# Filter spectra spread over two projections, both forget gates projected before the values, three logarithms in a row, residual rows kept in PSUM behind the experts

## The chip, the cores and the metric

The kernel runs on one core of one Trainium2 chip, in one launch with float32 inputs and outputs. The metric is the device time of one execution in microseconds. Engines are named as the profile names them: PE is TensorE, DVE is VectorE, ACT is ScalarE, POOL is GpSimd and SP is the queue of SyncE that issues nearly all weight loads.

## The reference, cut to what matters

Two blocks follow one another on 256 tokens of width 1024. The change touches the first block only.

```python
h = concat([meta_tokens(16), x(256)])              # 272 rows
p = rms_norm(h) @ w_in                             # 8 column groups of 512
y_hy = hyena_mixer(p[:, :1536])                    # groups 0 to 2: short convolution, then two long ones
y_hg = hgrn2_mixer(p[:, 1536:])                    # q, f_fwd, f_bwd, values, g
h = h + concat([rms_norm(y_hy), y_hg]) @ w_out
h = h + hier_moe(rms_norm(h))                      # 64 experts, top 2, weights of 6 MB each
h = rms_norm(h)                                    # then the second block, two layers

# filter of one long convolution, as a spectrum
filt = (sin(...) @ w3) * window                    # 272 taps, forward and backward; the 0th taps are summed
spec = rfft(two_sided(filt))
# forget gate of one direction
f = lb + (1 - lb) * sigmoid(logit);  k = 1 - f;  lf = log(f)
```

## The kernel before, in words

**Projections.** The mixer (`_phase_a`) multiplies in float32 by splitting each operand into a high and a low part and adding three products. A weight tile of 128x8x512 (2 MB) is loaded by `_load_w` into a ring buffer, and `_split_w` makes the pair for one of its 8 chunks: ACT writes the high part (L183) and DVE the low part (L184). The pairs lie in four buffers named `wp`. `hyena_proj(i)` makes column group i turned, in four PSUM tiles `mh`, with 96 matmuls of 272 columns, and its convolution then takes one ACT and two DVE instructions for each of the four tiles (L352 to L354). `tok_proj` makes a group token by token (tiles `mm`), with 48 matmuls of 512 columns, and 16 more where the meta tokens are wanted.

**Filter spectra.** The loop at L397 runs for both convolutions. For each of three chunks of taps (the 16 odd taps first) and both halves there are two matmuls into a PSUM tile `fl`, one DVE multiplication with the window `wn` (L412), one ACT copy and one DVE subtraction (L414, L415; the odd taps go by L420 to L425). Five rows of the spectrum then take 7 matmuls each, the last one 14, and an ACT copy into `H`. One filter is 54 matmuls of 512 columns.

**Order.** The framework assigns instructions to each engine's queue from a priority by program order and a time plan made when the program is built. Each queue then runs strictly in the order written, and `_after` pins an instruction behind another one. In program order the steps are: group 0, both filters, group 1, `to_freq` and group 2, first inverse transform, `to_freq`, forward gate (`forget_proj(0)`), second inverse transform, q, `pss` (a sum of squares), values v, release of the left half of the SBUF (`left.close()`), backward gate (`forget_proj(1)`), four `core` calls of the recurrence, `g_proj`, `out_proj(0)`, `out_proj(1)`.

**Ring buffers.** Until `left.close()` all weight tiles share one ring of three buffers. `early()` then opens a second ring of two, `ring2`, and puts it in front, so that the next loads take ring2, ring2, ring, ring, ring. `_moe` sets its own order, [r, r2, r2, r3, r3, r, r], and loads 11 of the first expert group's 12 tiles (gate 0 to 3, up 0 to 3, down 0 to 3) in a chain in which each is pinned behind the one before it:

```python
first.append(load_g(x, 0, i, {3: spare[0], 4: spare[1], 9: spare[2], 10: spare[3]}.get(n)))
if n:
    _after(k, k.load, prev)
```

Gate 3, up 0, down 1 and down 2 have buffers of their own (`spare`). Gate 1 and gate 2 take ring2, up 3 and down 0 take the first ring.

**End of the experts.** In the last group of four experts the down projection runs in four parts with 14 warm-up matmuls on the identity behind each of the first three. `finish` then makes one product for each half row (tile `sc`), DVE adds it to the row `h` in SBUF (L1142), multiplies with the gain into `fan` (L1147, two of the four on POOL), ACT squares both (L1152), a few one-column instructions and a POOL power give the scale (L1155 to L1158), and DVE makes the normalised row `an` (L1169), which PE turns (`tp`, L1175) for the next projection `pt`.

Of the kernel before, what the change touches and what calls it, by code (L numbers as in the profile page):

```python
# [8 lines left out]
F32 = mybir.dt.float32  # L9
# [29 lines left out]
def _consts():  # L39
# [24 lines left out]
    z = np.concatenate([tt[:, None], np.cos(ang), -np.sin(ang)], 1).astype(f)  # L64
    zt = np.ascontiguousarray(z[perm].T)
    deltas = np.abs(np.linspace(math.log(1e-2) / 1.5, math.log(1e-2) / 0.3, W, dtype=f))
    win = np.exp((-tt[:, None] * deltas[None, :]).astype(np.float64)).astype(f)[perm]

    om = 2.0 * math.pi * (np.arange(L1) + 0.5) / NDFT
    px, pm = np.arange(NM, L1), np.arange(NM)  # L70
# [94 lines left out]
def _load_w(k, src, rows=8, t=None, parts=1, between=None):  # L165
    if t is None:
        p = k.rings.pop(0)
        k.rings.append(p)
        t = p.tile([128, 8, 512], F32, name="wring")
    dst = t if rows == 8 else t.rearrange("p (k m) n -> p k (m n)", k=rows)  # L170
    n = rows // parts
    for i in range(0, rows, n):
        k.load = k.nc.sync.dma_start(dst[:, i:i + n], src[:, i:i + n])
        if between and i in between:
            between[i]()
    return t
# [25 lines left out]
def _phase_a(k, A, early):  # L202
# [180 lines left out]
    first = norms[0]  # L383
    behind = filt[-1][1]

    nc.sync.dma_start(wn, A["c_win"])


    H = [pa.tile([128, 5, W], F32, name=f"H{o}") for o in range(2)]
    wz.append(_load_w(k, win_ap[:, :, W:2 * W]))  # L390
    load_w3(1)
    k.load_c1()
    sks = [sp.tile([80, W], F32R, name=f"sk{i}") for i in range(2)]
    for sk in sks:
        G.memset(sk.bitcast(F32), 0.0)
        _after(k, nc.scalar.copy(sk, sk.bitcast(F32)), ends[0])
    for o in range(2):  # L397
        if o:

            later = w3_sums(o)  # L400
            w3_pair()
        sd = [[sp.tile([128, 2, W], F32R, name=f"sd{n}{i}") for n in "hl"] + [sks[i]] for i in range(2)]
        tm = []
        for kt in (2, 0, 1):
            n = 128 if kt < 2 else NM
            for i, (sh, sl, sk) in enumerate(sd):
                ks = slice(kt * 128, kt * 128 + n)
                p = px([128, W], "fl")
                _mm(k, p[:n], hids[:, ks], wsh[:, i], True, False)
                _mm(k, p[:n], hids[:, ks], wsl[:, i], False, True)  # L410
                t = sp.tile([128, W], F32, name="sdt", bufs=2)
                V.tensor_tensor(t[:n], p[:n], wn[:n, kt], op=OP.mult)  # L412
                if kt < 2:
                    nc.scalar.copy(sh[:, kt], t)  # L414
                    V.tensor_tensor(sl[:, kt], t, sh[:, kt].bitcast(F32), op=OP.subtract)  # L415
                else:
                    tm.append(t)
            if kt == 2:

                V.tensor_tensor(tm[0][0:1], tm[0][0:1], tm[1][0:1], op=OP.add)  # L420
                V.tensor_scalar(tm[0][0:1], tm[0][0:1], 0.5, None, op0=OP.mult)
                for (sh, sl, sk), t in zip(sd, tm):
                    nc.scalar.copy(sk[0:16], t[:16])
                    nc.scalar.copy(sk[32:48], t[:16])
                    V.tensor_tensor(sk[64:80], t[:16], sk[0:16].bitcast(F32), op=OP.subtract)  # L425
        for r in range(5):
            m = 128 if r < 4 else 64
            p = px([128, W], "fl")
            parts = [(sd[r // 2], r * 128)] if r < 4 else [(sd[0], 512), (sd[1], 576)]
            for i, ((sh, sl, sk), c0) in enumerate(parts):  # L430
                c = slice(c0, c0 + m)
                for kt in range(2):
                    _mm3(k, p[:m], (Fs[:, 0, kt, c], Fs[:, 1, kt, c]), (sh[:, kt], sl[:, kt]), i + kt == 0, False)
                _mm(k, p[:m], Fss[:, c], sk, False, i == len(parts) - 1)
            nc.scalar.copy(H[o][:m, r], p[:m])

    Fm = const(pa, "fm", [128, 2, 640], later)
    Fms = const(pa, "fmst", [80, 576], later)
# [101 lines left out]
    zk = hc.tile([80, W], F32R, name="zk")  # L540
    G.memset(zk.bitcast(F32), 0.0)
    nc.scalar.copy(zk, zk.bitcast(F32))
    hyena_proj(1)

    nw = hp.tile([128, W], F32, name="nw")
    k.bcast(nw, A["hgrn_norm"])
# [10 lines left out]
    def bound(n):  # L557

        l = VC[n].rearrange("p (r c) -> p r c", r=2)
        e, m = hp.tile([128, 2, 4], F32, name="lbe"), hp.tile([128, 4], F32, name="lbm")  # L560
        V.tensor_tensor(m, l[:, 0], l[:, 1], op=OP.max)
        for r in range(2):
            V.tensor_tensor(e[:, r], l[:, r], m, op=OP.subtract)
        nc.scalar.activation(e, e, AF.Exp)
        V.tensor_tensor(m, e[:, 0], e[:, 1], op=OP.add)
        V.reciprocal(m, m)
        V.tensor_tensor(m, m, e[:, 0], op=OP.mult)
        dg = hp.tile([128, 4, 128], F32, name="dg", tag="fe")
        V.tensor_tensor(dg, k.ident[:, None, :].to_broadcast([128, 4, 128]), m[:, :, None].to_broadcast([128, 4, 128]), op=OP.mult)
        p = px([128, 4, 128], "lb")  # L570
        for c in range(4):
            _mm(k, p[:, c], k.one, dg[:, c], c == 0, c == 3)
        p = p.rearrange("p a b -> p (a b)")
        lb = hp.tile([128, 2, W], F32, name="lb")
        for r, sg in enumerate((0.5, -0.5)):
            nc.scalar.activation(lb[:, r], p, AF.Copy, scale=sg, bias=0.5)
        return lb

    def forget(p, n, lb, ko, fo):
        e = hp.tile([n, W], F32, name="fe")  # L580
        nc.scalar.activation(e, p, AF.Tanh, scale=0.5)
        V.tensor_tensor(e, e, lb[:n, 1], op=OP.mult)
        V.tensor_tensor(fo, lb[:n, 0], e, op=OP.add)
        V.tensor_tensor(ko, lb[:n, 1], e, op=OP.subtract)

    def forget_proj(d):
        lb = bound(("lb_fwd", "lb_bwd")[d])
        P = tok_proj(hcols(1 + d), d == 0)
        for t in range(2):
            forget(P[t], 128, lb, kk[d][:, t], lf[d][:, t])  # L590
        if d == 0:
            meta_sum(mk, P[2])
            forget(mk, NM, lb, mk, ml)
            x = nc.scalar.activation(ml, ml, AF.Ln)
        y = nc.scalar.activation(lf[d], lf[d], AF.Ln)
        if d == 0:
            _after(k, y, x)

    Y = to_freq(uT[0], H[0])
    hyena_proj(2)  # L600
    for m in range(4):
        p = from_freq(Y, m)
        u = uT[0][:, m]
# [10 lines left out]
    for m in range(4):  # L614
# [6 lines left out]
        gc = VC["hyena_norm"][:, m:m + 1]  # L621
        nc.scalar.activation(hyT[0][:, m], y, AF.Copy, scale=gc)
        V.scalar_tensor_tensor(hyT[1][:, m], y, gc, hyT[0][:, m].bitcast(F32), op0=OP.mult, op1=OP.subtract)
    P = tok_proj(hcols(0), False)
    for t in range(2):
        e = _sigmoid(k, hp, P[t], W, tag="fe")
        V.tensor_tensor(q[:, t], P[t], e, op=OP.mult)
    pss = ps.tile([128, 2], F32, name="pss", tag="mm")
    for m in range(4):
        for t in range(2):  # L630
# [3 lines left out]
    V.tensor_copy(sst, pss)  # L634
    _rsqrt_mean(k, rh, sst, W, po, tag="rsh")

    P = tok_proj(hcols(3), True)
    for t in range(2):
        nc.scalar.copy(v[:, t], P[t])
    meta_sum(mv, P[2])  # L640
    hy1.close()
    left.close()
    psA.close()
# [168 lines left out]
            logits(1, n, range(4))  # L812
            squares(1, n)

    forget_proj(1)

    p = px([128, W], "ep")
    _mm(k, p[:NM], B3[0][2][32:48, 32:48].bitcast(F32), ml, True, True)
# [59 lines left out]
def _moe(k, A, ctx, ps):  # L878
# [230 lines left out]

    def finish(gT, y):


        fan = k.mp.tile([128, 2, D], F32, name="fan", tag="hn")
# [20 lines left out]
        k.pre = P, pairs  # L1136

        def scatter(t, n):
            p = ps.tile([128, W], F32, name="sc", tag="px")
            m = q(_mm(k, p, gT[:, t], y[n], True, True))  # L1140
            hs = k.h[:, t, n * W:(n + 1) * W]
            q(V.tensor_tensor(hs, p, hs, op=OP.add))  # L1142
            return m

        def gained(eng, t, n):
            cs = slice(n * W, (n + 1) * W)
            q(eng.tensor_tensor(fan[:, t, cs], k.h[:, t, cs], k.gains[:, 1, cs], op=OP.mult))  # L1147

        def squares(t, n):
            for j, src in enumerate((k.h, fan)):  # L1150
                sq = mo.tile([128, W], F32, name="nsq")
                q(ACT.activation(sq, src[:, t, n * W:(n + 1) * W], AF.Square, scale=D ** -0.5, accum_out=f(t, 2 * j + n)))  # L1152

        def scale(t):
            q(V.tensor_scalar(f(t, 5), f(t, 0), f(t, 1), EPS, op0=OP.add, op1=OP.add))  # L1155
# [29 lines left out]
                q(_mm(k, P[t], k.ahl[0][:, 1, c, HS(t)], pairs[i][0][:, j], False, c == 7))  # L1185

        scatter(0, 0)
        gained(V, 0, 0)
        scatter(0, 1)
        gained(V, 0, 1)  # L1190
        scatter(1, 0)
        q(warm_up(WS, scatter(1, 1), "mm"))
        squares(0, 0)
        squares(0, 1)
        gained(G, 1, 0)
        scale(0)
        hi(0)
        squares(1, 0)
# [2 lines left out]
        hi(1)  # L1201
        turned(0)
        mm(0, 0)
        gained(G, 1, 1)
        lo(1)
        mm(0, 1)
        hi(2)
# [9 lines left out]
        for t in range(2):  # L1217
            q(G.tensor_tensor(f(t, 4), f(t, 5), k.mhalf, op=OP.pow))
            q(ACT.activation(k.h[:, t], fan[:, t], AF.Copy, scale=f(t, 4)))

    JS = [slice(j * SLOTS, (j + 1) * SLOTS) for j in range(EP)]
    extra = {4: (0, 0), 6: (0, 1), 8: (1, 0), 10: (1, 1)}
    for g in range(k.ngroups):
# [55 lines left out]
        hT = mb.tile([128, 4, 128], F32, name="hT")  # L1279
        nc.scalar.copy(hT, p)  # L1280
        P = [ps.tile([128, W], F32, name="dn", tag="mm") for _ in range(2)]
        wm = None
        for f in range(4):
            for n in range(2):
                for j in range(EP):
                    m = _mm(k, P[n][JS[j]], hT[:, f, JS[j]], w(2, f, j, n), f == 0, f == 3)
                    if wm:
                        _after(k, m, wm)
            if g == k.ngroups - 1 and f < 3:
                wm = warm_up(WD, m, "px")  # L1290
        y = [mb.tile([128, W], F32, name="ye") for _ in range(2)]
        for n in range(2):
            (V.tensor_copy if n else nc.scalar.copy)(y[n], P[n])  # L1293
        if g == k.ngroups - 1:
            finish(gT, y)
            return
        for t in range(2):
            for n in range(2):
# [862 lines left out]
```

## Time and profile before

| what | value |
|---|---|
| median of 3 runs | 2095.82 us (2094.42 to 2096.31) |
| profiled execution: time | 2094.49 us |
| profiled execution: span | 2092.7 us |
| instructions | 24267 |
| PE busy | 1847.5 us, 88% |
| DVE busy | 919.5 us, 44% |
| ACT busy | 652.1 us, 31% |
| DMA | 593.92 MB, mean 284 GB/s |
| mean granted TensorE clock | 0.945 of full speed |

The span runs from the first to the last instruction on the core. Times inside it are counted from its start. Busy shares are averages over three stages: the mixer up to about 260 us, the experts from there to about 1200 us, and the second block to the end.

### The profile page before, as it was taken

Reading aid. Unit: us, or ns where it says so; the run is one execution under the profiler, and the core shown is the slowest. Engines: PE = TensorE matmul, PEld = TensorE weight load, DVE = VectorE, ACT = ScalarE, POOL = GpSimd, SP = SyncE. Lnnn points to the kernel's source line nnn. Section 1 sums busy time; section 2 is a strip of 40 time slices with the busy share of each in tenths; the row PEclk is TensorE's granted clock in tenths of the full one; section 3 lists DMA queues with packets and bytes.
Section 4 is the critical chain, followed back from the end, with each engine's and each line's share of the span. In section 5 each row is a group of like instructions: output and inputs, shape, how many; then the busy total and the mean of one; then the engine's idle time right before and its main releaser. Section 6 shows DMA issues by size and latency. Waiting matters only on the chain.

```text
span 2092.7 us, 24267 instructions
## 1 busy us (share of the span) xinstructions
PE 1847.5 (88%) x10132; PEld 1212.4 (58%) x10132; DVE 919.5 (44%) x1521; ACT 652.1 (31%) x976; POOL 69.6 (3%) x89
## 2 busy tenths in 40 slices
PE   8999987678787787876777799999999999999998
PEld 7877832224232331322222379898788788888886
DVE  6886621021111100111111176756666957756756
ACT  5556400002000100000000154546544645446444
POOL 2000000000000000000000020000000100000000
PEclk9999998789899998988988899999999999999999
DMA  8244899999999999999999954455454355454541
GB/s 278 95 159 146 305 398 428 424 404 415 428 423 428 424 427 428 423 427 423 428 426 428 392 182 161 161 180 182 167 185 166 133 190 179 165 180 171 178 159 55
DMA packets 123265, 593.92 MB, mean 284 GB/s; under 512 B 5951, under 2 KB 7264, under 8 KB 101008
## 3 DMA queue, kind: packets, MB, share of 16 engines
q1 hardware_dynamic: 119008, 583.66, 70.3%
q10 hardware_dynamic: 3376, 5.45, 0.8%
q0 software_dynamic: 768, 3.21, 0.4%
q8 instruction: 82, 1.34, 0.3%
q14 instruction: 31, 0.25, 0.0%
HBM read 591.26 MB, written 1.05 MB: 283 GB/s over the span
## 4 chain that ended last, share of the span: by engine, by line
PE 55%; DMA 21%; DVE 3%; issue 1%; ACT 1%; POOL 0%; ACTq 0%; SPq 0%; DVEq 0%; POOLq 0%
PE pt L141 23%; PE gu L141 10%; DMA wring<-in_w_up 8%; DMA wring<-in_w_down 7%; DMA wring<-in_w_gate 6%; PE pT L141 5%; PE pu L141 5%; PE dn L141 5%; PE pw L141 1%; PE ca L141 1%; DVE wp L184 1%; PE ov L141 1%; PE mk L141 1%; PE xp L141 1%; PE warm L141 0%
## 5 line engine op out<-in xcount | busy, mean ns | idle before, releaser
L141 PE MATMUL pt<-wp,ahl 128*128 128x512 f32 x2160 | 516.8, 397 | 1.7 <-DVE wp L184 1.7
L184 DVE TENSOR_TENSOR wp<-wring,wp 128x1024 fp32r<-128x1024 f32 (+1 forms) x368 | 405.7, 1112 | 238.5 <-ACT wp L183 231.2
L183 ACT ACTIVATE wp<-wring 128x1024 fp32r<-128x1024 f32 (+1 forms) x368 | 353.1, 966 | 350.5 <-PE pt L141 176.5
L141 PEld LDWEIGHTS pt<-wp,ahl 128*128 128x128 f32 x2160 | 403.2, 188 | 93.6 <-DVE wp L184 2.5
L141 PE MATMUL gu<-wring,xg 128*32 128x512 f32 x2016 | 322.4, 680 | 122.9 <-DMA wring<-in_w_up 101.3
L141 PEld LDWEIGHTS gu<-wring,xg 128*32 128x32 f32 x2016 | 75.0, 122 | 341.9 <-issue 163.7
L141 PE MATMUL dn<-wring,hT 128*32 128x512 f32 x992 | 186.0, 686 | 65.7 <-DMA wring<-in_w_down 49.9
L141 PEld LDWEIGHTS dn<-wring,hT 128*32 128x32 f32 x992 | 44.2, 118 | 194.2 <-issue 98.3
L1275 DVE SCALAR_TENSOR_TENSOR hh<-th,gu 128x512 f32<-128x512 f32 x16 | 16.9, 1055 | 308.5 <-PE gu L141 308.5
L1293 DVE COPY ye<-dn 128x512 f32<-128x512 f32 x16 | 11.1, 692 | 276.8 <-PE dn L141 276.8
L141 PEld LDWEIGHTS pT<-ahl,wp 128*128 128x128 f32 x960 | 115.6, 189 | 0.5
L141 PE MATMUL pT<-ahl,wp 128*128 128x256 f32 x960 | 115.8, 283 | 0.0
L1280 ACT COPY hT<-hp 128x512 f32<-128x512 f32 x16 | 9.4, 586 | 295.0 <-PE hp L1278 295.0
L141 PE MATMUL pu<-wp,yTh 128*128 128x512 f32 x320 | 98.9, 397 | 0.8 <-ACT yTh L1459 0.6
L1271 ACT ACTIVATE th<-gu 128x512 f32<-128x512 f32 x16 | 9.5, 596 | 250.5 <-PE gu L141 250.5
L1293 ACT COPY ye<-dn 128x512 f32<-128x512 f32 x16 | 9.4, 586 | 242.0 <-PE dn L141 242.0
L141 PEld LDWEIGHTS xp<-oh,hn 128*128 128x128 f32 x512 | 64.0, 200 | 31.1 <-issue 25.7
L141 PE MATMUL xp<-oh,hn 128*128 128x128 f32 x512 | 68.3, 288 | 7.8 <-PEq L1064 4.6
L141 PEld LDWEIGHTS pu<-wp,yTh 128*128 128x128 f32 x320 | 58.7, 188 | 15.6 <-ACT yTh L1459 3.5
L1272 DVE SCALAR_TENSOR_TENSOR th<-th,gu 128x512 f32<-128x512 f32 x16 | 11.0, 687 | 126.1 <-ACT th L1271 126.1
L141 PE MATMUL pu<-wp,yTl 128*128 128x512 f32 x160 | 61.0, 395 | 0.2
L141 PE MATMUL sc<-ye,gT 128*128 128x512 f32 x128 | 59.3, 606 | 0.0
(539 smaller groups left out, 1995.8 us busy)
## 6 DMA issues: line engine op xcount, KB each, us to landing
wring<-in_w_up SPq DMA_DIRECT2D x73, 2048.0 KB, 18.5
wring<-in_w_in SPq DMA_DIRECT2D x63, 2048.0 KB, 7.8
wring<-in_w_gate SPq DMA_DIRECT2D x63, 2048.0 KB, 19.4
wring<-in_w_down SPq DMA_DIRECT2D x62, 2048.0 KB, 20.9
wring<-in_w_out SPq DMA_DIRECT2D x6, 2048.0 KB, 7.9
wring<-in_w_mem_kv SPq DMA_DIRECT2D x4, 2048.0 KB, 17.0
spare<-in_w_down SPq DMA_DIRECT2D x2, 2048.0 KB, 9.6
wring<-in_w_in SPq DMA_DIRECT2D x4, 512.0 KB, 6.2
```

The costliest lines, as they stand in the source:

```text
L141: return k.nc.tensor.matmul(out, a, b, start=start, stop=stop, skip_group_check=True, **kw)
L183: ih = k.nc.scalar.activation(hi, w[:, a:b], AF.Copy)
L184: il = (eng or k.nc.vector).tensor_tensor(lo, w[:, a:b], hi.bitcast(F32), op=OP.subtract)
L1271: nc.scalar.activation(th, P[0], AF.Tanh, scale=0.5)
L1272: V.scalar_tensor_tensor(th, th, 1.0, P[0], op0=OP.add, op1=OP.mult)
L1275: V.scalar_tensor_tensor(hh, by_f(th), 0.5, by_f(P[1]), op0=OP.mult, op1=OP.mult)
L1280: nc.scalar.copy(hT, p)
L1293: (V.tensor_copy if n else nc.scalar.copy)(y[n], P[n])
```

## The change

- The 0th window value is halved in the constant, and the instruction that halved the sum of the 0th taps goes. The window is loaded behind group 1's weights instead of ahead of them, in two parts, without the rows that are empty.
- The loop over the filters becomes `filter_steps(o)`, eight pieces (three chunks of taps, now with the odd ones last, and five rows). `hyena_proj(1)` runs one piece of filter 0 at each of its 8 chunks, `hyena_proj(2)` one of filter 1.
- q's projection moves ahead of the first inverse transform, and both `bound` calls ahead of it. `forget_proj(1)` moves ahead of v, and `pss` behind v.
- `forget` computes (tanh - 1) times half of 1 - lb, then f = 1 + e and k = -e. `bound` makes one tile instead of two.
- The three logarithms run in a row behind the last tanh.
- In the last expert group, four matmuls on the identity put the rows of `h` into PSUM (`waiting_rows`), in place of eight warm-up matmuls in each of two parts. `finish` adds its products to them there, and `fan` and the squares read PSUM. All four `fan` products run on DVE.

```diff
-    nc.sync.dma_start(wn, A["c_win"])
     wz.append(_load_w(k, win_ap[:, :, W:2 * W]))
+    nc.sync.dma_start(wn[:, :2], A["c_win"][:, :2])
+    nc.sync.dma_start(wn[:NM, 2], A["c_win"][:NM, 2])
...
-    for o in range(2):
-        if o:
-
-            later = w3_sums(o)
-            w3_pair()
+    def filter_steps(o):
...
-                V.tensor_scalar(tm[0][0:1], tm[0][0:1], 0.5, None, op0=OP.mult)
...
+        steps = [lambda kt=kt: taps(kt) for kt in (0, 1, 2)] + [lambda r=r: row(r) for r in range(5)]
+        return dict(enumerate(steps))
+
+    hyena_proj(1, filter_steps(0))
+
+    later = w3_sums(1)
+    w3_pair()
+    hyena_proj(2, filter_steps(1))
...
-        lb = hp.tile([128, 2, W], F32, name="lb")
-        for r, sg in enumerate((0.5, -0.5)):
-            nc.scalar.activation(lb[:, r], p, AF.Copy, scale=sg, bias=0.5)
+        lb = hp.tile([128, W], F32, name="lb", bufs=2)
+        nc.scalar.activation(lb, p, AF.Copy, scale=-0.5, bias=0.5)
...
-        V.tensor_tensor(e, e, lb[:n, 1], op=OP.mult)
-        V.tensor_tensor(fo, lb[:n, 0], e, op=OP.add)
-        V.tensor_tensor(ko, lb[:n, 1], e, op=OP.subtract)
+        V.scalar_tensor_tensor(e, e, 1.0, lb[:n], op0=OP.subtract, op1=OP.mult)
+        V.tensor_scalar(fo, e, 1.0, None, op0=OP.add)
+        V.tensor_scalar(ko, e, -1.0, None, op0=OP.mult)
...
     Y = to_freq(uT[0], H[0])
-    hyena_proj(2)
+    lbs = [bound(n) for n in ("lb_fwd", "lb_bwd")]
+    P = tok_proj(hcols(0), False)
+    for t in range(2):
+        e = _sigmoid(k, hp, P[t], W, tag="fe")
+        V.tensor_tensor(q[:, t], P[t], e, op=OP.mult)
...
+    x = forget_proj(1)
+    for a in (ml, lf[0], lf[1]):
+        x = _after(k, nc.scalar.activation(a, a, AF.Ln), x)
+
+    P = tok_proj(hcols(3), True)
     for t in range(2):
-        e = _sigmoid(k, hp, P[t], W, tag="fe")
-        V.tensor_tensor(q[:, t], P[t], e, op=OP.mult)
+        nc.scalar.copy(v[:, t], P[t])
+    meta_sum(mv, P[2])
     pss = ps.tile([128, 2], F32, name="pss", tag="mm")
...
-    forget_proj(1)
...
         def scatter(t, n):
-            p = ps.tile([128, W], F32, name="sc", tag="px")
-            m = q(_mm(k, p, gT[:, t], y[n], True, True))
-            hs = k.h[:, t, n * W:(n + 1) * W]
-            q(V.tensor_tensor(hs, p, hs, op=OP.add))
-            return m
+            return q(_mm(k, rows[t, n], gT[:, t], y[n], False, True))
...
+    def waiting_rows(rows, t, behind):
+
+        for n in range(2):
+            p = rows[t, n] = ps.tile([128, W], F32, name="sc", tag="px")
+            behind = _after(k, _mm(k, p, k.ident, k.h[:, t, n * W:(n + 1) * W], True, False), behind)
+        return behind
...
             if g == k.ngroups - 1 and f < 3:
-                wm = warm_up(WD, m, "px")
+                if f < 2:
+                    m = waiting_rows(rows, f, m)
+                wm = warm_up(WD if f == 2 else WD - 8, m, "mm")
```

## Rows read from the trace of the kernel before

**Rows 1.** The page, 40 slices of the span: DMA's busy share in tenths, GB/s.

```profile
DMA  8244899999999999999999954455454355454541
GB/s 278 95 159 146 305 398 428 424 404 415 428 423 428 424 427 428 423 427 423 428 426 428 392 182 161 161 180 182 167 185 166 133 190 179 165 180 171 178 159 55
```

**Rows 2.** Busy time by stretches: PE, PEld, DVE, ACT, POOL, clock, DMA share, GB/s.

```profile
29.70:76.60 46.90, 41.54 (x208) 32.41 (x206) 30.61 (x56) 26.75 (x45) 5.17 (x7) 0.93 0.44 144
...
100.00:120.00 20.00, 20.00 (x100) 15.17 (x99) 18.82 (x41) 6.92 (x15) 0.52 (x1) 1.00 0.36 132
...
162.00:171.00 9.00, 9.00 (x40) 7.23 (x39) 3.94 (x7) 4.77 (x9) 0.00 (x0) 1.00 0.39 132
```

**Rows 3.** PE's waits, 29 to 230: us in total, times, longest.

```profile
PE fl L141 <- ACT sdh L414: 4.6, 2, 4.0
PE mm L141 <- ACT wp L183: 1.9, 1, 1.9
PE lb L141 <- DVE dg L569: 0.8, 1, 0.8
```

**Rows 4.** DVE's groups, 0 to 262: count, busy us, mean ns, idle before.

```profile
L184 DVE TENSOR_TENSOR wp<-wring,wp 128x512 fp32r<-128x512 f32 x80 | 53.4, 683 | 16.1 <-ACT wp L183 9.8 <-PE mm L141 6.1
L412 DVE TENSOR_TENSOR sdt<-fl,wn 128x512 f32<-128x512 f32 (+1 forms) x12 | 7.9, 676 | 7.2 <-PE fl L141 7.2
L353 DVE SCALAR_TENSOR_TENSOR uT<-mh,vecs,uT 128x271 f32<-128x271 f32 x12 | 5.8, 494 | 1.7 <-ACT uT L352 1.5
...
L197 DVE TENSOR_SCALAR fe<-fe 128x512 f32<-128x512 f32 x4 | 1.7, 436 | 0.3 <-ACT fe L196 0.3
```

**Rows 5.** ACT in order of time, 177 to 184: start, us.

```profile
177.42 1.28 ACT L595 ACT_TABLE_LOAD   x1
178.72 1.06 ACT L595 ACTIVATE lfb<-lfb 128x1024 f32<-128x1024 f32 x1
...
180.76 1.28 ACT L681 ACT_TABLE_LOAD   x1
```

**Rows 6.** Loads issued by SP in order of time: start, us to the last one's issue.

```profile
142.60 0.34 SPq L2117 DMA_DIRECT2D wr<-in_w_router  x1
142.99 1.19 SPq L173 DMA_DIRECT2D wring<-in_w_in  x2
151.49 39.81 SPq L173 DMA_DIRECT2D wring<-in_w_gate  x3
...
222.88 6.62 SPq L173 DMA_DIRECT2D wring<-in_w_up  x3
...
266.86 11.24 SPq L173 DMA_DIRECT2D wring<-in_w_gate  x4
```

**Rows 7.** DVE in order of time: the last low part of `out_proj(0)`'s weights.

```profile
228.42 0.69 DVE L184 TENSOR_TENSOR wp<-wring,wp 128x512 fp32r<-128x512 f32 x1
```

**Rows 8.** Busy time by stretches: DMA (last two columns) around the first expert loads.

```profile
220.00:270.00 50.00, 47.61 (x335) 38.63 (x337) 30.46 (x94) 18.70 (x41) 3.73 (x5) 1.00 0.80 301
230.00:240.00 10.00, 9.19 (x44) 7.24 (x43) 7.56 (x15) 4.58 (x8) 0.53 (x1) 1.00 1.03 414
191.00:192.00 1.00, 1.00 (x6) 0.79 (x6) 0.00 (x0) 0.00 (x0) 0.00 (x0) 1.00 0.11 12
```

**Rows 9.** End of the experts in order of time on PE, DVE and POOL.

```profile
1180.95 3.39 PE L141 MATMUL warm<-ident 128*128 128x128 f32 x28
...
1196.47 3.72 PE L141 MATMUL sc<-ye,gT 128*128 128x512 f32 x8
...
1205.15 1.78 PE L1175 MATMUL tp<-ident,an 128*128 128x128 f32 x8 [2.27 <-DVE an L1169]
...
1198.36 0.69 DVE L1147 TENSOR_TENSOR fan<-h,gains 128x512 f32<-128x512 f32 x1
...
1203.34 2.41 DVE L1169 SCALAR_TENSOR_TENSOR an<-fan,fs,gains 128x512 f32<-128x512 f32 x2 [0.65 <-POOL fs L1158]
...
1203.27 1.27 POOL L1147 TENSOR_TENSOR fan<-h,gains 128x512 f32<-128x512 f32 x1
```

More of the change, by code (lines that the diff above doesn't have):

```diff
@@ L66, in _consts @@
     deltas = np.abs(np.linspace(math.log(1e-2) / 1.5, math.log(1e-2) / 0.3, W, dtype=f))
-    win = np.exp((-tt[:, None] * deltas[None, :]).astype(np.float64)).astype(f)[perm]
+    win = np.exp((-tt[:, None] * deltas[None, :]).astype(np.float64)).astype(f)
+    win[0] *= f(0.5)
+    win = win[perm]
     om = 2.0 * math.pi * (np.arange(L1) + 0.5) / NDFT
@@ L396, in _phase_a, with taps @@
         _after(k, nc.scalar.copy(sk, sk.bitcast(F32)), ends[0])
-    for o in range(2):
-        if o:
-            later = w3_sums(o)
-            w3_pair()
+    def filter_steps(o):
         sd = [[sp.tile([128, 2, W], F32R, name=f"sd{n}{i}") for n in "hl"] + [sks[i]] for i in range(2)]
-        tm = []
-        for kt in (2, 0, 1):
+        def taps(kt):
             n = 128 if kt < 2 else NM
+            tm = []
             for i, (sh, sl, sk) in enumerate(sd):
@@ L425, in _phase_a, with row @@
                     V.tensor_tensor(sk[64:80], t[:16], sk[0:16].bitcast(F32), op=OP.subtract)
-        for r in range(5):
+        def row(r):
             m = 128 if r < 4 else 64
@@ L542, in _phase_a @@
     nc.scalar.copy(zk, zk.bitcast(F32))
-    hyena_proj(1)
     nw = hp.tile([128, W], F32, name="nw")
@@ L559, in bound @@
         l = VC[n].rearrange("p (r c) -> p r c", r=2)
-        e, m = hp.tile([128, 2, 4], F32, name="lbe"), hp.tile([128, 4], F32, name="lbm")
+        e, m = hp.tile([128, 2, 4], F32, name="lbe", bufs=2), hp.tile([128, 4], F32, name="lbm", bufs=2)
         V.tensor_tensor(m, l[:, 0], l[:, 1], op=OP.max)
@@ L580, in forget @@
         e = hp.tile([n, W], F32, name="fe")
-        nc.scalar.activation(e, p, AF.Tanh, scale=0.5)
-        V.tensor_tensor(e, e, lb[:n, 1], op=OP.mult)
-        V.tensor_tensor(fo, lb[:n, 0], e, op=OP.add)
-        V.tensor_tensor(ko, lb[:n, 1], e, op=OP.subtract)
+        x = nc.scalar.activation(e, p, AF.Tanh, scale=0.5)
+        V.scalar_tensor_tensor(e, e, 1.0, lb[:n], op0=OP.subtract, op1=OP.mult)
+        V.tensor_scalar(fo, e, 1.0, None, op0=OP.add)
+        V.tensor_scalar(ko, e, -1.0, None, op0=OP.mult)
+        return x
     def forget_proj(d):
-        lb = bound(("lb_fwd", "lb_bwd")[d])
+        lb = lbs[d]
         P = tok_proj(hcols(1 + d), d == 0)
         for t in range(2):
-            forget(P[t], 128, lb, kk[d][:, t], lf[d][:, t])
+            x = forget(P[t], 128, lb, kk[d][:, t], lf[d][:, t])
         if d == 0:
@@ L593, in forget_proj @@
             forget(mk, NM, lb, mk, ml)
[L594 to L597, printed above, removed]
+        return x
     Y = to_freq(uT[0], H[0])
-    hyena_proj(2)
+    lbs = [bound(n) for n in ("lb_fwd", "lb_bwd")]
[3 more added lines that the diff above has]
+        V.tensor_tensor(q[:, t], P[t], e, op=OP.mult)
     for m in range(4):
@@ L623, in _phase_a @@
         V.scalar_tensor_tensor(hyT[1][:, m], y, gc, hyT[0][:, m].bitcast(F32), op0=OP.mult, op1=OP.subtract)
-    P = tok_proj(hcols(0), False)
+    x = forget_proj(1)
+    for a in (ml, lf[0], lf[1]):
+        x = _after(k, nc.scalar.activation(a, a, AF.Ln), x)
+    P = tok_proj(hcols(3), True)
     for t in range(2):
-        e = _sigmoid(k, hp, P[t], W, tag="fe")
-        V.tensor_tensor(q[:, t], P[t], e, op=OP.mult)
+        nc.scalar.copy(v[:, t], P[t])
+    meta_sum(mv, P[2])
     pss = ps.tile([128, 2], F32, name="pss", tag="mm")
@@ L635, in _phase_a @@
     _rsqrt_mean(k, rh, sst, W, po, tag="rsh")
[L637 to L640, printed above, removed]
     hy1.close()
@@ L1108, in overflow, with finish @@
                         V.scalar_tensor_tensor(hs, p, ge[:, t:t + 1], hs, op0=OP.mult, op1=OP.add)
-    def finish(gT, y):
+    def finish(gT, y, rows):
         fan = k.mp.tile([128, 2, D], F32, name="fan", tag="hn")
@@ L1138, in scatter, with gained @@
         def scatter(t, n):
-            p = ps.tile([128, W], F32, name="sc", tag="px")
-            m = q(_mm(k, p, gT[:, t], y[n], True, True))
-            hs = k.h[:, t, n * W:(n + 1) * W]
-            q(V.tensor_tensor(hs, p, hs, op=OP.add))
-            return m
-        def gained(eng, t, n):
+            return q(_mm(k, rows[t, n], gT[:, t], y[n], False, True))
+        def gained(t, n):
             cs = slice(n * W, (n + 1) * W)
-            q(eng.tensor_tensor(fan[:, t, cs], k.h[:, t, cs], k.gains[:, 1, cs], op=OP.mult))
+            q(V.tensor_tensor(fan[:, t, cs], rows[t, n], k.gains[:, 1, cs], op=OP.mult))
         def squares(t, n):
-            for j, src in enumerate((k.h, fan)):
+            for j, src in enumerate((rows[t, n], fan[:, t, n * W:(n + 1) * W])):
                 sq = mo.tile([128, W], F32, name="nsq")
-                q(ACT.activation(sq, src[:, t, n * W:(n + 1) * W], AF.Square, scale=D ** -0.5, accum_out=f(t, 2 * j + n)))
+                q(ACT.activation(sq, src, AF.Square, scale=D ** -0.5, accum_out=f(t, 2 * j + n)))
         def scale(t):
@@ L1187, in finish @@
         scatter(0, 0)
-        gained(V, 0, 0)
+        gained(0, 0)
         scatter(0, 1)
-        gained(V, 0, 1)
+        gained(0, 1)
         scatter(1, 0)
@@ L1194, in finish @@
         squares(0, 1)
-        gained(G, 1, 0)
+        gained(1, 0)
         scale(0)
@@ L1203, in finish @@
         mm(0, 0)
-        gained(G, 1, 1)
+        gained(1, 1)
         lo(1)
@@ L1281, in _moe @@
         P = [ps.tile([128, W], F32, name="dn", tag="mm") for _ in range(2)]
-        wm = None
+        wm, rows = None, {}
         for f in range(4):
@@ L1294, in _moe @@
         if g == k.ngroups - 1:
-            finish(gT, y)
+            finish(gT, y, rows)
             return
```

## Prediction

> **What bounds the kernel now.** I read the page's slices first. DMA moves 398 to 428 GB/s in every slice from the sixth (from 262 us) to the twenty-second, and 305 or less in the five before [rows 1]. So the experts are one stream of weights with no slack. A microsecond by which that stream starts later or earlier is a microsecond at its end, whatever PE does meanwhile. Behind the experts the second block is a sequence on PE, so a microsecond saved in `finish` counts in full.
>
> Next I read stretches of the mixer. From 100 to 120 PE is busy 20.00 of 20 us and DVE 18.82 [rows 2]: PE is the bound, DVE close behind. From 29.7 to 76.6, where the filters lie, PE is busy only 41.54 of 46.90 us and its clock is 0.93. The list of PE's waits says why: 4.6 us for `sdh`, 4.0 of them at once, then 1.9 for a weight split behind ACT and 0.8 for `dg` [rows 3].
>
> The third view is SP's order of loads. It shows what ties mixer and experts together. The three gate loads that begin at 151.49 end with the one at 190.9 (151.49 + 39.81 - 0.37), the three up loads that begin at 222.88 with up 3 at 229.1 [rows 6]. That is the moment at which DVE ends the last low part of `w_out` 0 (228.42 + 0.69 = 229.1) [rows 7]. A load waits at the head of SP's queue until its buffer's last reader is through.
>
> **The filters.** Idle 46.90 - 41.54 = 5.4 us; of the clock, 0.07 of 46.9 us is 3.3 us of full-speed work lost [rows 2]. The stall of 4 us disappears, since the odd taps, which kept DVE from `sdt`, now come last. A filter is 54 matmuls of 0.23 us (9.00 us hold 39) [rows 2], 12.5 us, and a projection's 96 at 272 of 512 columns take 11.8: the work is only mixed anew.
>
> New waits stand at two boundaries, where a projection's convolution and the next filter's taps fall together. There DVE needs 8 x 0.49 for the convolution, 3 x 0.68 for splits and 8 x 0.68 for two chunks of taps, 11.4 us, before the first row can run [rows 4]. It may start 2.2 us before PE ends the projection, as the four tiles finish one by one. PE meanwhile has 12 tap matmuls and 36 of the next projection, 2.8 + 4.4 = 7.2 us. 11.4 - 2.2 - 7.2 = 2.0 us of idle PE, at each. Bounds: 0.5 if the plan puts more of the projection first; 4.5 if the odd taps, or the next `w3_pair`, get ahead on DVE. Queued behind such an instruction are the splits, and PE waits for those.
>
> **Gates, q and logarithms.** The same matmuls run in another order under a PE that is full [rows 2]. The wait for `dg` (0.8) goes, since both `bound`s now run under q's matmuls. `forget` saves DVE 2 x (0.68 - 0.44) = 0.5 us, five times [rows 4], and `bound` saves two ACT copies. I count these at nothing because PE covers them; without that cover they are worth at most 2.5 us. The halved tap and the shorter window load are free in the same way, as DVE and the queue have room there; a late window would delay the taps by the 1.3 us of its 544 KB at 414 GB/s [rows 8], inside the 4.5.
>
> The logarithms: one of them stands between two table loads of 1.28 us in the first `core` [rows 5], and PE waits 1.9 us for the split behind them [rows 3]. Three in a row leave one load behind, which can fall under v's matmuls; I take the 1.9 as gained. The Trainium skill, "ScalarE: Activation LUTs", section "What ACT_TABLE_LOAD costs", adds a drain of 1.38 us to such a load, 2.66 us a switch. The trace has the logarithm 0.02 us behind the load's end, so it does not show one. By the page two switches would be worth 5.3 us, 3.4 more than I take, and the sum would be 2097.2.
>
> At the end of v there is a new hole. `pss` now stands behind v, and `left.close()`, `ring2` and g's weights behind `pss`. Before, `forget_proj(1)` covered this. g's tile needs 1.0 us to the first byte (issued at 190.9, 12 GB/s from 191 to 192) and 2.10 MB / 414 GB/s = 5.1 [rows 6, 8], then a split. For some 7 us PE has only `core`'s own chain. Lower bound 0, if `pss` slips in between v's matmuls; upper 4; I take 1.5. Elsewhere I allow 0.5 (0 to 1.5).
>
> **The ring, and the start of the stream.** This decides. Before, `ring2` takes the backward gate's weights and g's, the two loads at 142.99 [rows 6], and `w_out` 0 and 1 go to the first ring. Now the backward gate is loaded ahead of `early()`. So `ring2` takes g's weights and `w_out` 0. Gate 1 then waits for g's, and gate 2 for `w_out` 0's last split. Behind gate 2 stand, pinned in the chain, gate 3, up 0 to 3 and down 0 to 3. Before, gate 2 went at 190.9, and only up 3 and what followed waited until 229.1.
>
> Call X the end of `w_out` 0's last split. Before X = 229.1. From it come off the 5.4 and 3.3 of the filters, 0.8 and 1.9: 11.4. On it come S = 2.0 + 2.0 + 1.5 + 0.5 = 6.0. X = 229.1 - 11.4 + 6.0 = 223.7.
>
> Before, 301 GB/s x 50 us = 15.05 MB move from 220 to 270 [rows 8]: seven tiles of 2.097 MB (up 1 to 3, down 0 to 3) and 0.36 MB of constants. So the second group's bytes begin at 270.0. Now ten tiles and the constants, 21.33 MB, begin to move 1.0 us after X at 414 GB/s, 51.5 us. The second group's begin at X + 52.5. The stream starts X - 217.5 later: 223.7 - 217.5 = +6.2 us. The mixer's gain is spent, as the time in which DMA idled (0.80 busy from 220 to 270) [rows 8] is now needed for tiles that used to come early.
>
> The Trainium skill, "DMA: Bandwidth & Descriptors", section "Anatomy of one DMA", says that "any semaphore wait happens on the issuing sequencer before dispatch", so a waiting load holds all behind it. Up 3's wait agrees with it. [...]
>
> **`finish`.** The add on the way (1198.36 - 1197.6 = 0.7) goes, and with POOL's `fan` off the shared work the first `an`, which runs beside it from 1203.34 (2.41 for two, 0.69 for one of DVE's in `fan`), loses up to 1.0, and a small instruction 0.5 [rows 9]. That is 2.2 at `tp`. ACT then sets the pace, as its squares and splits stand ahead of the copies of `tp`, and two products of 0.69 join DVE's queue. I take 1.4, bounds 0.3 and 2.4. The four identity matmuls cost 3.72 / 4 = 0.93 each, two of them 1.9, in place of 8/14 of 3.39, also 1.9 [rows 9]: nothing.
>
> **Sum.** +6.2 - 1.4 = +4.8. The profiled execution's 2094.49 becomes 2099.3. It lies 1.33 below the median of the runs, so by the median 2095.82 + 4.8 = 2100.6; I say 2100.5.
>
> **Rivals.** First, the boundaries fill and `pss` slips in: S = 2.5, X = 220.2, +2.7 - 1.4 = +1.3, 2097.1. For it: a queue's order follows a plan that found fillers elsewhere (20.00 of 20). Against: DVE's 11.4 us are there.
>
> Second, on the faster side, one mechanism: the chain does not hang on `w_out` 0. If its splits end early, because the plan draws `out_proj(0)` ahead into the `core` calls by more than before, X falls, and the change breaks even at X = 217.5 + 1.4 = 218.9 and wins by 4.2 us, which can be measured, from X = 214.7 down. At X = 211.5 the stream starts 6.0 earlier, the sum is -6.0 - 1.4 = -7.4 and the time 2088.4. For it: before, the last product of `out_proj(0)`'s first half ran just behind the last `core`. Against: g's weights now come later, so the fillers do too.
>
> Third, the change does not do what it says: new holes as large as the old, the clock falling with one of 4 us as it did. S = 11.4, X = 229.1, +11.6 - 1.4 = +10.2, 2106.0.
>
> **How the numbers follow.** Forecast (X 222 to 227) 0.40, first rival 0.28, second 0.22, third 0.10. A measurement of this kernel tells some 0.2% from no change, 4.2 us: 2091.6 to 2100.0. Faster 0.22 is the second rival. The forecast's own range is 2098.9 to 2103.9 (X 222 to 227), and about a fifth of it lies within 0.2%: same 0.28 + 0.08 = 0.36, slower 0.32 + 0.10 = 0.42. For 8 in 10 the range runs from 2090.0 (X = 213, inside the second rival) to 2106.0, the third.
>
> **What would show it.** Right: gate 2 and the nine loads behind it issued from about 224 at once, DMA at 1.0 from there, the second group's first issue later than 266.86 or its tiles landing later, while PE's wait for `sdh` and the two table loads around the logarithm are gone. In `finish`, no add and `tp` about 1.4 us closer to `sc`. Wrong: gate 2 issued before 215; or DMA below full speed after it, which would mean that PE's progress and not the ring starts the stream.

## The result and the profile after

Median 2107.15 us (2106.37 to 2108.96, 6 runs) against 2096.07 us: ratio 1.0055, 95% interval 1.0042 to 1.0068, so 11.1 us slower. The forecast was 2100.5 in 2090.0 to 2106.0: the direction of the forecast, but beyond its range. The profiled execution has a span of 2104.8, 12.1 more than before.

First the page's slices after the change, for [rows 1].

```profile
DMA  9233699999999999999999954545454354454541
GB/s 307 66 113 121 234 412 428 427 424 399 428 424 428 426 425 428 423 428 428 428 425 424 411 189 175 183 160 170 173 207 159 127 200 164 166 191 170 173 161 57
```

The fifth slice (210 to 263 us) falls from 305 to 234 GB/s: the stream begins later. From the sixth on it is as full as before, so nothing is won back.

SP's loads after, start and time to the last one's issue, for [rows 6].

```profile
147.56 0.37 SPq L175 DMA_DIRECT2D wring<-in_w_gate  x1
167.70 0.34 SPq L2132 DMA_DIRECT2D wr<-in_w_router  x1
168.09 0.43 SPq L175 DMA_DIRECT2D wring<-in_w_in  x1
168.56 0.58 SPq L175 DMA_DIRECT2D wring<-in_w_out  x1
204.14 28.90 SPq L175 DMA_DIRECT2D wring<-in_w_gate  x2
233.13 0.46 SPq L175 DMA_DIRECT2D spare<-in_w_gate  x1
233.64 0.50 SPq L175 DMA_DIRECT2D spare<-in_w_up  x1
234.20 13.79 SPq L175 DMA_DIRECT2D wring<-in_w_up  x3
```

Gate 1 goes at 204.14. Gate 2 waits until 204.14 + 28.90 - 0.37 = 232.67, and gate 3 and the up loads follow at once. This is the chain of the prediction, 9 us later than it said. What it waits for is on DVE, in order of time:

```profile
231.37 1.28 DVE L186 TENSOR_TENSOR wp<-wring,wp 128x512 fp32r<-128x512 f32 x2
```

X = 231.37 + 1.28 = 232.65. So why is X late? PE's waits after the change, from 29 to 230 us (total, times, longest), for [rows 3], and stretches of its time, for [rows 2]:

```profile
PE up L143 <- DVE mkf L830: 3.6, 1, 3.6
PE mm L143 <- DVE wp L186: 3.2, 1, 3.2
PE tp L703 <- DVE qd L697: 1.4, 1, 1.4
PE mm L143 <- ACT wp L185: 1.2, 1, 1.2
PE mh L143 <- DVE wp L186: 0.8, 1, 0.8
```

```profile
29.70:80.30 50.60, 49.74 (x303) 42.48 (x302) 38.17 (x70) 30.68 (x53) 5.18 (x7) 1.00 0.58 196
90.00:105.00 15.00, 11.84 (x47) 9.27 (x46) 9.93 (x19) 3.61 (x6) 0.00 (x0) 0.77 0.10 22
165.00:185.00 20.00, 13.82 (x79) 10.94 (x78) 8.63 (x16) 10.76 (x19) 1.72 (x3) 0.74 0.60 224
...
95.00:100.00 5.00, 4.94 (x18) 3.98 (x19) 3.10 (x6) 0.60 (x1) 0.00 (x0) 0.50 0.00 0
...
170.00:175.00 5.00, 2.86 (x10) 2.28 (x10) 2.04 (x3) 0.30 (x1) 0.00 (x0) 0.50 1.04 393
175.00:180.00 5.00, 3.59 (x13) 2.68 (x12) 1.29 (x2) 2.62 (x5) 0.00 (x0) 0.55 1.04 411
```

In the filters PE idles 50.60 - 49.74 = 0.9 us at full clock, where it idled 5.4 at 0.93. But two new holes stand there: 3.2 us near 92 and 6.2 us from 165 to 185. At each the granted clock falls to the lower of its two levels (0.50 in 95 to 100 and in 170 to 175, which is 1.2 of 2.4 GHz). In steps of 5 us, PE's busy time times the share that the clock lacked adds another 3.1 us to the first hole (4.94 x 0.50 = 2.5 of it in 95 to 100) and 3.3 to the second (1.4 and 1.6 of it in the last two rows).

The first hole is the wait for a low part of q's weights. DVE and PE in order of time:

```profile
85.79 0.69 DVE L186 TENSOR_TENSOR wp<-wring,wp 128x512 fp32r<-128x512 f32 x1
86.40 0.68 DVE L522 TENSOR_TENSOR Y<-fz,H 128x512 f32<-128x512 f32 x1
...
93.59 0.67 DVE L528 TENSOR_TENSOR Y<-Y,yt 128x512 f32<-128x512 f32 x1
94.19 0.22 DVE L575 TENSOR_TENSOR lbm<-lbm,lbe 128x4 f32<-128x4 f32 x2
94.33 0.67 DVE L186 TENSOR_TENSOR wp<-wring,wp 128x512 fp32r<-128x512 f32 x1
```

```profile
91.27 0.63 PE L143 MATMUL mm<-wp,ah 128*128 128x512 f32 x2
95.06 0.80 PE L143 MATMUL mm<-wp,ah 128*128 128x512 f32 x1 [3.17 <-DVE wp L186]
```

Between two low parts stand the 13 products of the spectrum, 8 us in one piece, and ahead of them the convolution of group 2. The buffers `wp` hold only four pairs of weights; PE runs out of them at 91.9.

The second hole is the end of v. PE, then DVE:

```profile
165.79 1.84 PE L143 MATMUL pss<-tri,ysq 128*128 128x1 f32 x16
167.56 1.03 PE L143 MATMUL ep<-mkf,tri 16*16 16x512 f32 x2
172.14 2.07 PE L143 MATMUL up<-mv,mkf 16*128 16x128 f32 x8 [3.56 <-DVE mkf L830]
```

```profile
170.74 0.76 DVE L755 TENSOR_TENSOR wr<-wr,vecs 128x576 f32<-128x576 f32 x1 [1.54 <-DMA wr<-in_w_router]
171.42 0.67 DVE L830 TENSOR_TENSOR mkf<-mkf,ex 16x512 f32<-16x512 f32 x1
```

`pss` runs at 165.79, the load of `wr` goes at 167.70 and that of g's weights at 168.09. Until g's first pair is split PE has only the small products of the first `core`, each with a round over ACT and DVE; one of those DVE instructions, `mkf`, even stands behind a product that waits for `wr`. Its other operand `ex` is ready at 170.31 (ACT, 169.72 + 0.59), so by these rows that product costs some 1.1 of the 3.6 us.

`finish` after, on PE, for [rows 9]:

```profile
1195.73 1.98 PE L143 MATMUL sc<-h,ident 128*128 128x512 f32 x4
...
1211.12 3.73 PE L143 MATMUL sc<-ye,gT 128*128 128x512 f32 x8
1214.68 2.84 PE L143 MATMUL warm<-ident 128*128 128x128 f32 x24
1217.73 1.29 PE L1181 MATMUL tp<-ident,an 128*128 128x128 f32 x8 [0.21 <-DVE an L1175]
1219.67 2.16 PE L143 MATMUL pt<-wring,ahl 128*128 128x512 f32 x7 [0.65 <-ACT ahl L1183]
1222.72 4.28 PE L143 MATMUL pt<-wring,ahl 128*128 128x512 f32 x17 [0.89 <-DVE wring L1170]
...
1233.99 11.31 PE L143 MATMUL pt<-wp,ahl 128*128 128x512 f32 x48
```

From `sc` to `tp` it is 6.61 instead of 8.68 us, and 22.87 from `sc` to the `pt` with split weights (1220.74 - 1196.47 = 24.27 in the kernel before, in the same view): 1.4 us gained. The wait for `an` before `tp` is gone, and two shorter ones behind ACT and DVE have come.

### The profile page after: what moved, and what is told of

Read it like the earlier page. It is cut to its first block, busy times and chain, and to the rows that moved or that the text cites. A ratio compares the mean times of both kernels' runs of the same rounds, so it can differ in the third digit from the quotient of the medians.

```text
span 2104.8 us, 24222 instructions
## 1 busy us (share of the span) xinstructions
PE 1847.0 (88%) x10108; PEld 1211.5 (58%) x10108; DVE 913.0 (43%) x1517; ACT 649.4 (31%) x972; POOL 68.0 (3%) x87
## 4 chain that ended last, share of the span: by engine, by line
PE 55%; DMA 20%; DVE 2%; issue 1%; ACT 1%; POOL 0%; ACTq 0%; DVEq 0%; POOLq 0%; SPq 0%
PE pt L143 23%; PE gu L143 10%; DMA wring<-in_w_up 8%; DMA wring<-in_w_down 7%; DMA wring<-in_w_gate 6%; PE pT L143 5%; PE pu L143 5%; PE dn L143 5%; PE pw L143 1%; PE ca L143 1%; DVE wp L186 1%; PE ov L143 1%; PE xp L143 1%; PE mk L143 1%; PE sc L143 1%
## 5 line engine op out<-in xcount | busy, mean ns | idle before, releaser
L1308 DVE COPY ye<-dn 128x512 f32<-128x512 f32 x16 | 11.1, 692 | 275.3 <-PE dn L143 275.3
## 6 DMA issues: line engine op xcount, KB each, us to landing
wring<-in_w_mem_kv SPq DMA_DIRECT2D x4, 2048.0 KB, 16.6
```

## The experiments

Runs of one kernel scattered more on the chips of the experiments (the kernel before: 2091.44 to 2102.70 in 29 runs), so each is read by its interval and by marks inside its trace.

**The ring, with everything else as before.** In the kernel before, the backward gate's weights get a buffer of the first ring, so that `ring2` takes g's and `w_out` 0.

```diff
     def hcols(j):
+        if j == 2:
+            rg = [p for p in k.rings if p is not k.r2][0]
+            return _load_w(k, win_ap[:, :, 5 * W:6 * W], t=rg.tile([128, 8, 512], F32, name="wring"))
         return _load_w(k, win_ap[:, :, (3 + j) * W:(4 + j) * W])
```

> The kernel before, with the backward gate's weights in the first ring, so that ring2 takes g's weights and w_out 0 as after the change; no other edit. Theory A: PE's mixer ends as before, X stays at about 229, gate 2 and nine loads stand behind it, and by the prediction's formula the stream starts X - 217.5 = 11.6 us later: 2096 + 11.6 = 2107.7 (2104 to 2110). Rival B: the loads had slack, the time stays at 2096 within 1.

Measured 2109.21 us, ratio 1.0064 (1.0046 to 1.0082). Its profiled execution has a span of 2102.9, 10.2 more. SP and PE there:

```profile
151.80 77.70 SPq L173 DMA_DIRECT2D wring<-in_w_gate  x3
229.59 0.46 SPq L173 DMA_DIRECT2D spare<-in_w_gate  x1
```

```profile
261.14 1.92 PE L141 MATMUL gu<-wring,xg 128*32 128x512 f32 x16 [0.44 <-DVE xg L1251]
```

Gate 2 goes at 229.1 instead of 190.9, and PE's first expert product is where it was (261.16 before), yet the stream of weights and all behind it run some 11 us later. The choice of one buffer costs about as much as the whole change. Rival B is out.

**The ring repaired in the changed kernel.**

```diff
-    w += [_load_w(k, wo[h], 4) for h in range(2)]
+    rg = [p for p in k.rings if p is not k.r2][0]
+    w += [_load_w(k, wo[h], 4, rg.tile([128, 8, 512], F32, name="wring")) for h in range(2)]
```

> The changed kernel, with both tiles of w_out in the first ring, so that gate 2 waits for g's weights and not for w_out 0. Theory A (a pinned chain of loads behind the last split of w_out 0): of the 14.7 us by which the stream of expert weights runs later after the change, 7.2 are PE's (first expert product at 268.35 instead of 261.16) and about 7.5 the chain's. Gate 2 is issued near 204, gate 3 and up 0 to 2 before 233, and the time falls by 7.5 to about 2099.6 (2097 to 2102). Rival B (only PE's late mixer sets the stream): gate 2 goes early too, but the time stays at 2107 within 1.

2100.53 us, ratio to before 1.0018 (1.0007 to 1.0030): 4.6 us over the kernel before on its chip, where the changed kernel is 11.1 over. That is the size that A gave, but the cause is not as clean as the number. Gate 2 goes early, at 207.5; yet the plan put `core` and g's products in another order, and PE came to its first expert product 3.6 us later still (271.98 instead of 268.35), with gate 3 at 228.3. The clock has a part in that: it stays at the lower level from 170 to 190 us, where the changed kernel has full clock again at 180, and loses 8.8 us there instead of 3.3. The chain behind `w_out` 0 is gone; that PE's lateness sets what is left of the delay fits the marks below, but no run shows it alone.

**The first hole.**

```diff
-            wh, wl = _split_w(k, w, s, s + QS)
+            wh, wl = _split_w(k, w, s, s + QS, G if s in pooled else None)
...
-    P = tok_proj(hcols(0), False)
+    P = tok_proj(hcols(0), False, (3, 4, 5))
```

> The changed kernel, with the low parts of chunks 3 to 5 of q's weights made on POOL instead of DVE. Theory A: the wait of 3.17 us for a low part at 95 and most of the 3 us lost at half clock behind it go; X and with it the stream come 5.6 us earlier, 2107.1 - 5.6 = 2101.5 (2100 to 2104). Rival C: the waits at the end of v and in core are set by something else and grow by what is gained here, 2106 to 2108. Rival D: POOL's low parts come later than DVE's would, the wait moves and the time is 2107 or more.

2101.77 us, 1.0028 (1.0016 to 1.0039) of before: 5.9 us over it, 5.2 less than the changed kernel, as A expected. The wait of 3.2 us is gone from PE's list, PE is busy without a break from 88 to 106 at full clock, and X is 228.1, 4.5 earlier (5.6 said).

**The second hole.** The load order stays that of the changed kernel, only the filler comes back.

```diff
-    x = forget_proj(1)
-    for a in (ml, lf[0], lf[1]):
-        x = _after(k, nc.scalar.activation(a, a, AF.Ln), x)
+    for a in (ml, lf[0]):
+        x0 = _after(k, nc.scalar.activation(a, a, AF.Ln), x0)
+    wb = hcols(2)
...
+    x = forget_proj(1, wb)
+    _after(k, nc.scalar.activation(lf[1], lf[1], AF.Ln), x)
     p = px([128, W], "ep")
```

> The changed kernel, with the backward gate's projection behind the release of the left half again (its weights are loaded ahead of v's projection as after the change, its logarithm follows it; the other two logarithms stand where they were). The order of loads and rings is that of the changed kernel. Theory A (the holes of 6.2 us and the 3.3 us of clock from 165 to 185 are what the missing filler costs, and the chain behind w_out 0 hands them on): X from 233.1 to 223.6, time 2107.1 - 9.5 = 2097.6 (2095.5 to 2100). Rival B (core's own chain or the late pss sets that stretch): the waits stay, 2104 to 2107.

2098.99 us, 1.0014 (1.0004 to 1.0024) of before: 2.5 us over it, 8.5 less than the changed kernel; A had 9.5. From its trace, the stretch of the second hole, and loads:

```profile
165.00:185.00 20.00, 18.43 (x108) 14.32 (x107) 13.72 (x28) 14.60 (x23) 0.00 (x0) 1.00 0.27 94
```

```profile
181.39 42.81 SPq L175 DMA_DIRECT2D wring<-in_w_gate  x2
224.26 0.50 SPq L175 DMA_DIRECT2D spare<-in_w_gate  x1
```

PE is busy 18.43 instead of 13.82 us, at full clock. This run also decides between the chain and PE: its first expert product begins at 255.84, 5.3 us **earlier** than before, and its stream still runs 5.7 us **later** (below), as gate 2 waited until 223.8.

**Parts of the change on the kernel before.** First only the filters in pieces (the diff of the change, without gates, q and `finish`):

> The kernel before, with only the filters in pieces in the projections of groups 1 and 2, the halved window and its later load. Theory A: PE's idle time in the filters falls from 5.4 to about 0.9 us and the 3.3 us of clock come back, X comes 7.8 us earlier and so do the first expert product and the stream, as the ring is unchanged: 2096 - 7.8 = 2088.3 (2086 to 2091). Rival B: the gain is lost again in waits before the experts, 2094 to 2097. Rival E: the boundaries between projection and filter cost 2.0 us each as predicted, 2092.

2092.69 us, 0.9988 (0.9975 to 1.0001): 3.2 of the 7.8 us expected, and by the interval not told from zero. PE in its trace:

```profile
131.27 1.01 PE L143 MATMUL pss<-tri,ysq 128*128 128x1 f32 x4 [2.10 <-ACT ysq L628]
```

The filters' idle time went as hoped (0.8 us are left). But a new hole of 2.1 us stands at `pss`, whose last squares are on ACT behind the forward gate's logarithm and its table load, and the clock fell behind it (2.9 us more). The expectation was wrong by a wait that the change itself moves away. The stream came 5.9 us early all the same; 3.6 of these were lost again in the experts (below).

Then only `finish` with the rows in PSUM:

> The kernel before, with only the rows of h in PSUM behind the experts and finish that goes with them. Theory A: the 1.5 us between the first product of finish and the first product with split weights that the changed kernel shows (13.2 against 14.65 us later than before) come alone too: 2096 - 1.5 = 2094.5 (2093.5 to 2095.5). Rival B: the gain is lost behind it or in the four identity products ahead, 2096.

2095.17 us, 0.9992 (0.9983 to 1.0001): 1.3 us, by the interval not told from zero. What shows the gain is the trace: 22.88 us from `sc` to the `pt` with split weights, as in the changed kernel.

**Versions that beat both.** The kernel before with the filters in pieces, `finish`, and the two logarithms pinned behind the last copy `hyTh`:

> The kernel before, with the filters in pieces, the two logarithms of the forward gate pinned behind the last copy of the second inverse transform, and the rows in PSUM behind the experts; rings, gates and order else as before. Theory A: before_filters lost 2.1 us and 2.9 us of clock where pss waited for a square that stood behind the logarithm on ACT; without that the first expert product comes 7.8 us earlier than before, and finish gives 1.5: 2096 - 9.3 = 2086.7 (2084 to 2089.5). Rival B (the stream gives back what PE gains): 2091 or more.

2088.54 us, 0.9952 (0.9938 to 0.9965). The time came, but not by the mechanism: `pss` still waits 1.0 us (for a square that now stands behind DVE's `y`), the clock is 0.89 from 125 to 140 and 0.85 from 165 to 185, and the first expert product is only 1.1 us early. From 25 to 260 us, in steps of 5, PE idles 7.4 us instead of 10.6, but loses 6.5 us of clock instead of 2.8. Of these, 5.0 stand behind the wait of 1.9 us for a split in the first `core`, which the kernel before has too, at full clock. The 5 us behind it, here:

```profile
180.00:185.00 5.00, 5.00 (x27) 4.76 (x26) 2.40 (x7) 0.69 (x3) 0.00 (x0) 0.50 0.00 0
```

And in the kernel before:

```profile
185.00:190.00 5.00, 5.00 (x50) 4.74 (x50) 4.41 (x13) 1.48 (x4) 0.00 (x0) 1.00 0.02 5
```

Its profiled execution, with a span of 2087.4, gained 5.3 us, of which 2.7 lie behind `sc`.

And the changed kernel with all three repairs:

```diff
+    wv = hcols(3)
+    wb = hcols(2)
...
-            k.rings, k.r3 = [r, k.r2, k.r2, r3, r3, r, r], r3
+            k.rings, k.r3 = [k.r2, k.r2, r, r3, r3, r, r], r3
```

> The changed kernel with three repairs: the backward gate's projection behind the release of the left half, low parts of chunks 3 to 5 of q's weights on POOL, both tiles of w_out in the first ring (gate 0 and 1 in ring2, gate 2 in the first). Theory A: of after's first expert product, 7.2 us late, 6.2 and 9.5 go, so that it comes 8.5 us earlier than before; no load waits for w_out 0 ahead of up 3; with finish 2096 - 8.5 - 1.5 = 2086 (2083 to 2090). Rival B: q ahead of the first inverse transform and the late pss cost more than the closed holes, 2092 or more.

2081.35 us, 0.9927 (0.9913 to 0.9940), 15 us faster than before, 5 more than A expected. Its first expert product is 10.2 us early instead of 8.5, and `finish` and what lies behind it gave 2.3 instead of 1.5 in its profiled execution. That execution, with a span of 2080.5, is 12.2 us shorter; the other 3 of the 15 us no trace shows. PE loses no clock at all from 25 to 260 us. Its loads, and its first expert product:

```profile
151.06 27.02 SPq L175 DMA_DIRECT2D wring<-in_w_gate  x3
194.77 0.37 SPq L175 DMA_DIRECT2D spare<-in_w_gate  x1
```

```profile
250.97 1.92 PE L143 MATMUL gu<-wring,xg 128*32 128x512 f32 x16 [0.45 <-DVE xg L1266]
```

**All marks side by side.** X is when the split that holds gate 2 back ends. The stream's mark is the issue of the first `mem_kv` load (462.90 in the kernel before). Differences to the kernel before, us:

| kernel | X - 217.5 | first expert product | stream |
|---|---|---|---|
| changed | 15.2 | +7.2 | +15.1 |
| before, ring as changed | 11.6 | 0.0 | +11.2 |
| changed, q's low parts on POOL | 10.6 | +2.7 | +10.4 |
| changed, gate late | 6.3 | -5.3 | +5.7 |
| changed, ring repaired | none | +10.8 | +8.8 |
| before, filters only | none | -3.6 | -5.9 |
| before, `finish` only | none | +1.2 | +0.4 |
| before, filters, `finish`, logarithms pinned | none | -1.1 | -2.4 |
| changed, three repairs | none | -10.2 | -9.9 |

"None" means that gate 2 does not wait for `w_out` 0. The row with `finish` only, whose mixer has no edit, shows by how much such marks differ between two traces: some 1 us. Where the chain stands behind `w_out` 0, the stream follows X - 217.5 within 0.6 us, whatever PE does. Where it doesn't, the stream follows PE's first expert product, within 2.3 us. In the four of these kernels whose rows lie below the repaired ring, up 3 still waits for the last split of `w_out` 0, and the end of that split has moved by as much as PE's product (for the three repairs 218.95 instead of 229.11, 10.2). Which of the two starts their stream these runs do not tell apart.

From the stream's mark to `sc` eight of the ten kernels took 733.1 to 733.6 us in their profiled executions, the one with the filters only 737.2 and the one with `finish` only 738.4. The edit of `finish` lies at the end of this stretch, but the changed kernel has it too, at 733.1. What slowed the experts in these two executions the runs do not show; their times hold it.

## Why the prediction was right in kind and wrong in size

**The ring and the formula: right.** X - 217.5 gives 15.2 for the changed kernel, and the stream is 15.1 late; four kernels lie on that line within 0.6. (The prediction counts down 3, the last of the nine loads, as pinned in the chain; it only follows in the queue.) The Trainium skill, "DMA: Bandwidth & Descriptors", section "Anatomy of one DMA", lets a semaphore wait happen on the issuing sequencer before dispatch. The traces agree: gate 2's issue and the end of the split lie within 0.05 us of each other in all four kernels, and what stood behind it went then.

**`finish`: right.** 2.1 us at `tp` (2.2 said) and 1.4 behind it (1.4 said). Another 1.1 came with it: in the second block the waits for `sc` at `ov` (another tile of that name) fell from 1.8 to 0.5 us in the changed kernel's profile, and so in the one with `finish` alone. The prediction did not have that, and by which path `finish` does it is not shown.

**The filters: right in what goes, too dear in what comes.** 5.4 us of idle time became 0.9, the clock stayed at full. At the boundaries PE waited 0.83 and less than 0.1 us, not 2.0 each.

**The logarithms: right.** ACT loads its tables three times from 29 to 262 us instead of five, and PE's wait of 1.9 us went. The load ahead of the logarithms fell under v's matmuls, as said; the one behind them (168.42 to 169.70, ahead of `ex`) stands in the second hole, where `wr` came later still. The first of these two loads ends at 154.48 and the logarithm starts at 154.50, so here too no row shows the drain that the Trainium skill, "ScalarE: Activation LUTs", section "What ACT_TABLE_LOAD costs", adds.

**The step that failed is S, the new stalls, said to be 6.0 us and measured at 16.6:** 0.9 at the boundaries, 3.2 and 3.1 at the first hole, 6.2 and 3.3 at the second, before rounding. It failed at two terms.

"Gates, q and logarithms" got no stall of its own, because "The same matmuls run in another order under a PE that is full". It cost 3.2 us and 3.1 of clock; only the 0.5 of "elsewhere" stood against that. A full PE in the old order showed only that the old order had a projection beside each transform, with pairs already split. In the new one DVE had the convolution of group 2 and the spectrum product in one run, and q's next low part behind them. With that low part on POOL the hole went.

"At the end of v" I took 1.5 (0 to 4): it cost 6.2 us and 3.3 of clock. There the text named the right thing, 7 us in which PE has only `core`'s own chain, and then priced it far below that for no row that said so. With the gate's projection back in its place PE idled 1.6 us there, at full clock.

Neither term had a clock in it, though [rows 2] showed what a hole does to it.

With the measured S the working gives X = 229.1 - 11.4 + 16.6 = 234.3, 1.6 above what was found. In steps of 5 us the filters' lost clock is 2.8 and not the 3.3 that the prediction took off, so the gap is rather 2.1; where it comes from stays open. 15.1 late, with 0.4 less at `sc`, 1.4 less behind `finish` and 1.1 less in the second block is 12.2, and the spans differ by 12.1. The third rival had S = 11.4 and 2106.0: the right kind, still too small.

What stays open too is why the clock fell in the version with the two logarithms pinned, where it stayed full in the kernel before.

## What to carry to other kernels

When a step moves, write down what it covered at the place that it leaves, and price that hole whole, with the clock behind it; "the engine is full there" describes the old order, not the new one. Follow each buffer of a ring through the new order of loads: in a pinned chain one tile that waits for a late reader holds back everything behind it, and that can cost as much as all the compute around it. A gain ahead of such a wait is only worth what the wait lets through, so repair the chain first and measure then.

## What the hardware showed that was not expected

What the clock took at a hole did not go by the hole's length. In steps of 5 us, PE's busy time times the share that the clock lacked:

| hole of PE | kernel | lost clock, us |
|---|---|---|
| 1.9 us, a split behind ACT in the first `core` | before; before, filters only | 0.0 |
| the same | before, filters, `finish`, logarithms pinned | 5.0 |
| 2.1 us, `pss` | before, filters only | 2.9 |
| 3.2 us, q's low part | changed | 3.1 |
| the same | changed, gate late; changed, ring repaired | 1.6 |
| 6.2 us, the end of v | changed | 3.3 |
| 5.3 us there | changed, ring repaired | 8.8 |

Each kernel has one profiled execution here, so the 6.4 us of clock in S belong to one execution. What sets two equal holes apart these runs do not show.
